# Pinning VectorE and TensorE to program order around the context's last rows, and starting the second matrix's GpSimd sums with the third feed pair

## The chip, the cores and the metric

The kernel runs on one core of one Trainium2 chip. The metric is the device time of one execution in microseconds (us). Before the change three runs gave 1945.74, 1946.46 and 1949.13 us; the median is 1946.46 us. One more execution was taken with the hardware profiler on.

The engines go by the profile's names: PE is the matrix engine (TensorE), PEld its weight loads, DVE is VectorE, ACT is ScalarE, POOL is GpSimd, SP is SyncE, which here only issues transfers. ACT and POOL issue transfers too.

## The reference

One layer of a diffusion backbone works on 1024 latent tokens and 256 context tokens, both 1024 channels wide. The change touches only the end of the first half and the feed-forward block:

```python
x = x + gt1 * (merged @ w_out)
u2 = rmsnorm(x, g_norm2) * (1 + sc2) + sh2
x = x + gt2 * (jnp.square(jax.nn.relu(u2 @ w_ff1)) @ w_ff2)
```

Here `w_out` is 1024 x 1024, `w_ff1` is 1024 x 4096 and `w_ff2` is 4096 x 1024, all in float32. The scales, shifts and gates (`sc2`, `sh2`, `gt1`, `gt2`) differ between context and latent tokens.

## The kernel before

**Numbers in two halves.** Every matrix operand is split into a rounded half `h` and a rest `l`. ACT casts the `h`; DVE subtracts to get the `l`. Each product is then three matmuls: `h·h`, `h·l`, `l·h`. A split of one 128 x 512 tile is thus one ACT cast and one DVE subtraction.

**Tokens.** The ten row tiles of 128 tokens form three groups: group 0 (tiles 0 to 3), group 1 (tiles 4 to 7), both latent, and group 2 (tiles 8 and 9), the context.

**Output projection.** `project_out` (L1158) forms, for one row tile and one range of columns, 24 matmuls into a PSUM bank `po`. DVE multiplies by the gate (L1171) and adds to the rows `z` (L1173); ACT squares the sum and leaves a row sum in `fsq` (L1174). For the context the columns come in four quarters `q` of 256. `context_out(q)` (L1178) first fetches and splits four weight tiles (`raw_wc`, `hi_wc`, `lo_wc`; L879 to L882), then calls `project_out` for tiles 8 and 9. The raw tiles have 4 buffers (`first4`), the `h` halves 6 (`six`) and the `l` halves 6 (`ring`).

**Normalised columns.** `modulate_ff(g)` (L1118) sums `fsq` (DVE, `fs`, L1122), makes the reciprocal root (`rs_f`: DVE L129, then POOL L130), scales the rows (`xn`: even tiles on ACT L1134, odd tiles on DVE L1136), transposes them on PE into PSUM (`pt`, L1142; five banks of the kind `sd`), and evicts. For groups 0 and 1 ACT evicts to `u2r` (L1151) and DVE splits some of them (`u2h`, `u2l`, L1154 and L1155). For the context ACT works inside PSUM (L1146), and DVE takes both halves from there (`u20c` to `u27c`: a cast at L1147 and a subtraction at L1148 for each of eight column blocks, two blocks to a quarter `qt`).

**Feed-forward, first matrix.** A `Pair` takes two of the 32 blocks of `w_ff1` and the latent tokens as a 2 x 2 block product with seven half-size products instead of eight. The right sides are four quarters of `u2`, `B11`, `B21`, `B12`, `B22`, and four sums of them, `T1` to `T4`. Each quarter has four tiles, `kk` = 0 to 3. `quarter_sums` (L780) overwrites the raw quarters by the sums, 4 DVE subtractions for each `kk`, and `split_sum` (L789, L790) splits them, 4 for each sum. A pair goes through `begin` (the products with `B11` and `B21`, `fB`), `contexts` (the context tokens, `fc`; it splits the quarters `a21` and `a22` of the weights), `rest` (DVE differences of weights at L947, splits `s_...` at L872 and L873, the products `fT` with `T4`, `T2`, `T3`, `T1` and one with `B22`) and `sums` (DVE L1227 to L1230, stores `scr_h`, `scr_c`, `scr_s`). In the profile `a_0l` is the `l` half of a weight quarter of pair 0, `s_0l` that of a difference. The raw weights of a pair lie in one of two places, so a pair's load (L905) waits for the last split of the pair two before it.

**Feed-forward, second matrix.** `second_sums(fp)` (L1235) makes the same kind of sums of `w_ff2`: two loads by SP into one place (`z` 16 to 19; L1239), four POOL subtractions (L1242), one store by POOL (`scr_t`, L1243). The next call's loads wait until that store has landed. The sums are read in the second half of the feed-forward block only.

**What sets the order.** The Tile framework puts the instructions of each engine in one fixed queue when the kernel is built. It takes them by readiness in a modelled run, and by program order among the ready. An engine's queue is then worked in that order, and an instruction that waits holds up all behind it. `Pinned(tc, engine)` (L33) is a wrapper that the kernel already uses in its first part: each instruction issued through it is put in the engine's queue behind the instruction that the program issued last on that engine, pinned or not. It orders the queue and adds no wait for that instruction's end. Instructions issued without the wrapper may still be placed anywhere between.

Around the change the program reads: `context_out(0)`, `context_out(1)`, `modulate_ff(1)`, `context_out(2)`, `context_out(3)`, then `begin` of pairs 0 and 1, `modulate_ff(2)`, all quarter sums, the splits in the order `T4`, `T3`, `T2`, `T1`, `contexts` of pairs 0 and 1, and then for each of 16 pairs `rest`, `sums` and `second_sums`, with no pinning.

Of the kernel before, what the change touches and what calls it, by code (L numbers as in the profile page):

```python
# [48 lines left out]
def hybrid_step(  # L49
# [1065 lines left out]

    fsq = cp.tile([P, NT, 4], F32, name="fsq")

    def modulate_ff(g):  # L1118
        t0, n = GROUPS[g]
        tiles = range(t0 // P, (t0 + n) // P)  # L1120
        fs = small([P, 4], f"fs{g}")[:, : len(tiles)]
        V.reduce_sum(fs, fsq[:, tiles[0] : tiles[-1] + 1, 0 : 4 if g == 2 else 2], axis=mybir.AxisListType.X)  # L1122
        r = rstd_of(fs, len(tiles), f"f{g}")

        j = 1 if g == 2 else 0
        for qt in range(4):
            xn = []
            for ii, i in enumerate(tiles):
                if ii % 2 == 0:
                    t = tmp2(f"xn{i}_{qt}")  # L1130
                v = t[:, (ii % 2) * 256 : (ii % 2) * 256 + 256]
                xv = xt[i][:, qt * 256 : (qt + 1) * 256]
                if ii % 2 == 0:
                    A.activation(v, xv, AF.Copy, scale=r[:, ii : ii + 1])  # L1134
                else:
                    V.tensor_scalar(v, xv, r[:, ii : ii + 1], None, ALU.mult)  # L1136
                xn.append(v)
            for kk in range(2):
                k = qt * 2 + kk
                ps = ps_sd(f"pt2{g}_{k}")  # L1140
                for ii in range(n // P):
                    PE.transpose(ps[:, ii * P : (ii + 1) * P], xn[ii][:, kk * P : (kk + 1) * P], ident)  # L1142
                if g == 2:
                    c = slot(f"u2{k}c")
                    u2c[k] = hi, lo = c[:, 0:256], c[:, 256:512]
                    A.activation(ps[:, :n], ps[:, :n], AF.Identity, bias=sh2[:, k, j : j + 1], scale=a2[:, k, j : j + 1])  # L1146
                    V.tensor_copy(hi, ps[:, :n])  # L1147
                    V.tensor_tensor(lo, ps[:, :n], hi.bitcast(F32), ALU.subtract)  # L1148
                    continue
                rf = raw2[g][k] = slot(f"u2r{k}_{g}", F32)  # L1150
                A.activation(rf, ps[:, :n], AF.Identity, bias=sh2[:, k, j : j + 1], scale=a2[:, k, j : j + 1])  # L1151
                if g == 0 or k >= 4:
                    hi, lo = slot(f"u2h{k}_{g}"), slot(f"u2l{k}_{g}")
                    V.tensor_copy(hi, rf)  # L1154
                    V.tensor_tensor(lo, rf, hi.bitcast(F32), ALU.subtract)  # L1155
                    u2s[f"B{1 + k // 4}{1 + g}", k % 4] = hi, lo

    def project_out(tiles, c0, n, weights):  # L1158

        for i in tiles:  # L1160
            g = min(i // 4, 2)
            o = i * P - GROUPS[g][0]
            full = ps_mm(f"po{c0}_{i}")
            ps = full[:, :n]
            for k in range(KT):
                whi, wlo = weights(k)
                mh, ml = mT[k][g]
                PE.matmul(ps, mh[:, o : o + P], whi, start=k == 0, stop=False)  # L1168
                PE.matmul(ps, ml[:, o : o + P], whi, start=False, stop=False)
                PE.matmul(ps, mh[:, o : o + P], wlo, start=False, stop=k == KT - 1)  # L1170
            V.tensor_tensor(ps, ps, gt1[(2 if g == 2 else 0) + c0 // 512][:, c0 % 512 : c0 % 512 + n], ALU.mult)  # L1171
            xc = xt[i][:, c0 : c0 + n]
            V.tensor_tensor(xc, xc, ps, ALU.add)  # L1173
            A.activation(ps, xc, AF.Square, accum_out=fsq[:, i, c0 // n : c0 // n + 1])  # L1174
            if c0 + n == D:
                SP.dma_start(scr_x[i], xt[i])

    def context_out(q):  # L1178
        ws = context_weights(q)
        project_out((8, 9), q * 256, 256, lambda k: tuple(w[:, k % 2 * 256 : k % 2 * 256 + 256] for w in ws[k // 2]))  # L1180

# [2 lines left out]
    project_out(range(5), 512, 512, lambda k: w_out1[k])  # L1186
    modulate_ff(0)
    project_out(range(5, 8), 512, 512, lambda k: w_out1[k])
    context_out(0)
    context_out(1)  # L1190
    modulate_ff(1)
    quarters = (("B11", 0, 0), ("B21", 0, 4), ("B12", 1, 0), ("B22", 1, 4))
    raw2q = {nm: raw2[g][o : o + 4] for nm, g, o in quarters}
    context_out(2)
    context_out(3)

# [43 lines left out]
            G.tensor_tensor(out, x, y, ALU.subtract)  # L1242
        G.dma_start(scr_t[fp], zs(16, 4).rearrange("p (q c) -> p q c", c=512))  # L1243


    pairs = {}

    def feed_pair(fp):
        odd = fp % 2
        pairs[fp] = FeedPair(  # L1250
            f"{fp}", fp, (w_ff1[2 * fp], w_ff1[2 * fp + 1]), 4 if odd else 0, range(8, 12) if odd else range(12, 16), u2s, u2c)

    for fp in (0, 1):
        feed_pair(fp)
        pairs[fp].begin()
    modulate_ff(2)
    quarter_sums(raw2q)
    for nm in ("T4", "T3", "T2", "T1"):
        split_sum(u2s, raw2q, nm)
    for fp in (0, 1):  # L1260
        pairs[fp].contexts()
    for fp in range(NFP):
        if fp not in pairs:
            feed_pair(fp)
            pairs[fp].begin()
            pairs[fp].contexts()
        pairs[fp].rest()
        pairs[fp].sums()
        del pairs[fp]
        second_sums(fp)  # L1270


    pa.close()
# [262 lines left out]
```

## Time and profile before

| | us |
|---|---|
| median of three runs | 1946.46 |
| the profiled execution's own time | 1947.31 |
| its span, first to last instruction | 1945.5 |
| PE busy in it | 1903.0 |
| DVE busy | 1294.0 |
| ACT busy | 861.7 |
| POOL busy | 378.2 |

The profiled execution's time exceeds its span by 1.8 us, and the median of the runs by 0.85 us. All times of instructions below count from the start of the span. The projection of the context's rows starts at 1118.5 us, the feed pairs begin at 1145.0 us, and the second matrix's products run from about 1556 us to the end.

### The profile page before, as it was taken

What the parts mean: (1) busy time and instruction counts of PE and PEld (TensorE: products, weight loads), DVE (VectorE), ACT (ScalarE), POOL (GpSimd) and SP (SyncE); (2) the same over time, 40 slices, a digit from 0 to 9 for tenths busy, and PEclk for the clock granted to TensorE, in tenths of its full rate; (3) what the DMA queues carried; (4) which work ended last, traced back from release to release, by engine and by line L of the source; (5) the groups of instructions that cost most, each with busy time, mean ns of one, the idle gap of its engine ahead of it and who ended that gap; (6) DMA issues with size and microseconds to landing.
All of it is one profiled execution on the core that took longest, in us unless ns stands there. A gap on an engine that the chain in (4) does not pass through costs nothing.

```text
span 1945.5 us, 28129 instructions
## 1 busy us (share of the span) xinstructions
PE 1903.0 (98%) x10136; PEld 1627.5 (84%) x10136; DVE 1294.0 (67%) x2207; ACT 861.7 (44%) x1768; POOL 378.2 (19%) x380
## 2 busy tenths in 40 slices
PE   6999999999999999999999999999999999999998
PEld 3778888998788888888888887888888888888886
DVE  6574443347759889875675599888776655744665
ACT  7444464653243333343123374555454545443443
POOL 1200001107302424220000015444431110000003
PEclk9999999999999999999999999999999999999999
DMA  9211111012635445469522435776773586654444
GB/s 361 85 59 33 43 39 40 27 56 70 203 119 165 149 158 164 153 211 321 163 97 98 152 120 212 253 264 246 259 269 136 193 333 203 210 170 151 165 133 159
DMA packets 149318, 313.32 MB, mean 161 GB/s; under 512 B 17550, under 2 KB 40818, under 8 KB 147130
## 3 DMA queue, kind: packets, MB, share of 16 engines
q1 hardware_dynamic: 107354, 220.73, 33.9%
q0 software_dynamic: 15520, 57.75, 7.8%
q10 hardware_dynamic: 26304, 33.04, 4.7%
q8 instruction: 79, 1.29, 0.3%
q14 instruction: 61, 0.50, 0.1%
HBM read 217.59 MB, written 93.36 MB: 160 GB/s over the span
## 4 chain that ended last, share of the span: by engine, by line
PE 87%; DVE 4%; DMA 3%; POOL 2%; ACT 1%; issue 1%; SPq 0%; POOLq 0%; ACTq 0%; DVEq 0%
PE w L1403 6%; PE w L1404 6%; PE w L1405 6%; PE pb L1050 3%; PE pb L1051 3%; PE pb L1052 3%; PE fT L892 3%; PE fT L890 3%; PE fT L891 3%; PE fB L891 2%; PE fB L890 2%; PE fB L892 2%; PE fT_g L892 2%; PE fT_g L890 2%; PE fT_g L891 2%; PE po L1168 2%
## 5 line engine op out<-in xcount | busy, mean ns | idle before, releaser
L1242 POOL TENSOR_TENSOR z<-z 128x512 f32<-128x512 f32 x64 | 100.1, 1564 | 123.3 <-DMA z<-in_w_ff 120.6
L947 DVE TENSOR_TENSOR z<-z 128x512 f32<-128x512 f32 x112 | 88.7, 792 | 2.5
L527 POOL PARTITION_ALL_REDUCE acc<-acc x16 | 54.6, 3446 | 184.0 <-DVE acc L521 113.6
L521 DVE SCALAR_TENSOR_TENSOR acc<-z,scond,acc 128x512 f32<-128x512 f32 x112 | 86.1, 816 | 0.0
L1357 POOL TENSOR_TENSOR rs_y<-rs_y,neghalf 128x1 f32<-128x1 f32 x10 | 9.6, 966 | 333.0 <-DVE rs_y L1356 333.0
L1208 ACT ACTIVATE z<-z 128x512 f32<-128x512 f32 x64 | 40.5, 632 | 69.8 <-DVE z L956 36.7
L972 ACT ACTIVATE z<-z 128x512 f32<-128x512 f32 x48 | 30.3, 632 | 59.1 <-DVE z L956 23.1
L130 POOL TENSOR_TENSOR rs_h<-rs_h,neghalf 128x4 f32<-128x4 f32 (+1 forms) x12 | 10.9, 910 | 200.5 <-DVE rs_h L129 200.3
L653 DVE SCALAR_TENSOR_TENSOR yc<-th,ccol,z 128x512 f32<-128x512 f32 (+1 forms) x12 | 7.9, 661 | 58.2 <-PE th L651 58.2
L1056 DVE TENSOR_TENSOR sg<-pb,sg 128x512 f32<-128x512 f32 (+1 forms) x48 | 28.7, 600 | 26.7 <-PE pb L1052 26.5
L881 ACT CAST hi_wb<-raw_wb 128x512 fp32r<-128x512 f32 x24 | 14.8, 620 | 64.4 <-PE pb L1051 37.6
L1209 ACT ACTIVATE z<-z 128x512 f32<-128x512 f32 x64 | 40.3, 629 | 1.1
L1171 DVE TENSOR_TENSOR po<-po,gt 128x512 f32<-128x512 f32 (+1 forms) x24 | 14.6, 607 | 35.1 <-PE po L1170 35.0
L1233 POOL DMA_DIRECT2D scr_s<-x x48 | 26.3, 549 | 53.1 <-DVE x L1227 47.6
L738 POOL TENSOR_TENSOR z<-z 128x1024 f32<-128x1024 f32 (+13 forms) x20 | 33.6, 1702 | 6.9 <-ACT z L722 4.6
L528 POOL TENSOR_TENSOR acc<-acc,bt 1x512 f32<-1x512 f32 x16 | 23.5, 1480 | 58.4 <-issue 58.4
L1174 ACT ACTIVATE po<-z 128x512 f32<-128x512 f32 (+1 forms) x24 | 12.7, 529 | 48.5 <-DVE z L1173 34.2
L587 DVE SCALAR_TENSOR_TENSOR z<-z,dmb,kv 128x129 f32<-128x129 f32 x56 | 16.6, 345 | 21.8 <-PE kv L576 21.3
L1057 DVE TENSOR_TENSOR z<-z,sg 128x512 f32<-128x512 f32 (+1 forms) x48 | 28.7, 601 | 1.2
L640 DVE TENSOR_TENSOR den<-den,gcol 128x2 f32<-128x2 f32 x40 | 6.2, 159 | 31.0 <-ACT den L639 29.9
L43 PE MATMUL pm<-wah,shl 128*4 128x512 f32 x32 | 13.8, 461 | 13.2 <-ACT wah L43 13.2
L130 POOL TENSOR_TENSOR rs_f<-rs_f,neghalf 128x4 f32<-128x4 f32 (+1 forms) x3 | 3.3, 1092 | 116.9 <-DVE rs_f L129 116.9
(5136 smaller groups left out, 7288.9 us busy)
## 6 DMA issues: line engine op xcount, KB each, us to landing
z<-in_w_ff SPq DMA_DIRECT2D x64, 512.0 KB, 5.5
z<-in_w_ada SPq DMA_DIRECT2D x64, 256.0 KB, 3.1
scr_t<-z POOLq DMA_DIRECT2D x16, 1024.0 KB, 4.9
z<-in_w_in SPq DMA_DIRECT2D x24, 512.0 KB, 4.3
scr_g<-z ACTq DMA_DIRECT2D x48, 256.0 KB, 2.0
sg<-scr_g SPq DMA_DIRECT2D x48, 256.0 KB, 4.5
scr_h<-z ACTq DMA_DIRECT2D x48, 256.0 KB, 3.6
scr_s<-x POOLq DMA_DIRECT2D x48, 256.0 KB, 4.3
```

The source lines that it names most:

```text
L521: V.scalar_tensor_tensor(acc[j], raw, scond[:, k, j : j + 1], acc[j], ALU.mult, ALU.add)
L890: PE.matmul(ps, whi[:, s], ahi, start=first and k == ks[0], stop=False)
L891: PE.matmul(ps, whi[:, s], alo, start=False, stop=False)
L892: PE.matmul(ps, wlo[:, s], ahi, start=False, stop=end and k == ks[-1])
L947: V.tensor_tensor(out, x, y, op)
L1050: PE.matmul(pb[:, :n], whi[:, s], yh, start=kc == 0, stop=False)
L1051: PE.matmul(pb[:, :n], whi[:, s], yl, start=False, stop=False)
L1052: PE.matmul(pb[:, :n], wlo[:, s], yh, start=False, stop=kc == 3)
L1242: G.tensor_tensor(out, x, y, ALU.subtract)
L1403: PE.matmul(banks[j], h_[:, s], rh, start=fp == 0, stop=False)
L1404: PE.matmul(banks[j], l_[:, s], rh, start=False, stop=False)
L1405: PE.matmul(banks[j], h_[:, s], rl, start=False, stop=fp == NFP - 1)
```

## The change

The calls after `modulate_ff(1)` are put in another order, and some are pinned:

1. The raw weights of pairs 0 and 1 and the context weights of quarters 2 and 3 are requested and split first, unpinned.
2. With DVE and PE pinned: the rows of `context_out(2)`, the quarter sums for `kk` = 0, the rows of tile 8 of `context_out(3)`, the sums for `kk` = 1, the rows of tile 9.
3. With PE alone pinned: `begin` of pairs 0 and 1.
4. With DVE alone pinned: `modulate_ff(2)`, in which the sums for `kk` = 2 stand between the reciprocal root and the scaling of the rows; then the sums for `kk` = 3; then the splits in the order `T4`, `T2`, `T3`, `T1`.
5. In the loop over pairs SP is pinned, and no `second_sums` is called for pairs 0 and 1; pairs 2 and 3 call it twice, later pairs once, so all 16 are made.

```diff
-    def modulate_ff(g):
+    def modulate_ff(g, between=None):
...
         r = rstd_of(fs, len(tiles), f"f{g}")
+        if between:
+            between()
...
-    def project_out(tiles, c0, n, weights):
+    def project_out(tiles, c0, n, weights, between=None):
         for i in tiles:
+            if between and i == tiles[-1]:
+                between()
...
-    context_out(0)
-    context_out(1)
+    for q in (0, 1):
+        context_out(q, context_weights(q))
     modulate_ff(1)
...
-    context_out(2)
-    context_out(3)
...
     for fp in (0, 1):
         feed_pair(fp)
+
+    def row_sums(kk):
+        b11, b21, b12, b22 = (raw2q[nm][kk] for nm in ("B11", "B21", "B12", "B22"))
+        for out, x, y in ((b11, b12, b11), (b12, b22, b12), (b22, b22, b11), (b21, b22, b21)):
+            V.tensor_tensor(out, x, y, ALU.subtract)
+
+    wcs = [context_weights(q) for q in (2, 3)]
+    V, PE = Pinned(tc, engines[0]), Pinned(tc, engines[3])
+    context_out(2, wcs[0])
+    row_sums(0)
+    context_out(3, wcs[1], lambda: row_sums(1))
+    V = engines[0]
+    for fp in (0, 1):
         pairs[fp].begin()
-    modulate_ff(2)
-    quarter_sums(raw2q)
-    for nm in ("T4", "T3", "T2", "T1"):
+    PE = engines[3]
+    V = Pinned(tc, engines[0])
+
+    modulate_ff(2, lambda: row_sums(2))
+    row_sums(3)
+    for nm in ("T4", "T2", "T3", "T1"):
         split_sum(u2s, raw2q, nm)
+    V = engines[0]
     for fp in (0, 1):
         pairs[fp].contexts()
+    SP = Pinned(tc, nc.sync)
+    summed = 0
     for fp in range(NFP):
...
-        second_sums(fp)
+        for _ in range(min(2, fp + 1 - summed) if fp > 1 else 0):
+            second_sums(summed)
+            summed += 1
+    SP = nc.sync
```

More of the change, by code (lines that the diff above doesn't have):

```diff
@@ L1176, in project_out, with context_out @@
                 SP.dma_start(scr_x[i], xt[i])
-    def context_out(q):
-        ws = context_weights(q)
-        project_out((8, 9), q * 256, 256, lambda k: tuple(w[:, k % 2 * 256 : k % 2 * 256 + 256] for w in ws[k // 2]))
+    def context_out(q, ws, between=None):
+        project_out((8, 9), q * 256, 256, lambda k: tuple(w[:, k % 2 * 256 : k % 2 * 256 + 256] for w in ws[k // 2]), between)
     project_out(range(8), 0, 512, lambda k: w_out0[k])
```

## The prediction

> **What bounds the kernel now.** I read the page's first section, then the busy times by stage, then PE's waits from the context's rows to the end, and last each engine's order around those waits.
>
> ```profile
> PE 1903.0 (98%) x10136; PEld 1627.5 (84%) x10136; DVE 1294.0 (67%) x2207; ACT 861.7 (44%) x1768; POOL 378.2 (19%) x380
> ```
>
> PE is busy for 98% of the span, and the change removes no matmul. It can only win back idle time of PE, or add some. The stages (span in us; busy us of PE, PEld, DVE, ACT, POOL; PE clock; DMA share; GB/s) show where that lies:
>
> ```profile
> 1118.00:1145.00 27.00, 27.00 (x228) 26.88 (x227) 24.96 (x54) 21.54 (x46) 1.52 (x1) 1.00 0.38 118
> 1145.00:1160.00 15.00, 11.97 (x54) 9.73 (x53) 13.24 (x28) 8.58 (x21) 0.70 (x1) 0.96 0.26 105
> 1160.00:1190.00 30.00, 27.91 (x165) 23.72 (x164) 29.26 (x51) 18.56 (x39) 17.73 (x8) 0.96 0.45 155
> 1190.00:1235.00 45.00, 42.65 (x210) 35.28 (x209) 39.93 (x55) 22.43 (x42) 21.66 (x24) 1.00 0.72 262
> 1235.00:1560.00 325.00, 325.00 (x1724) 281.16 (x1723) 242.08 (x357) 166.53 (x309) 118.11 (x134) 1.00 0.65 231
> ```
>
> PE has no idle time up to 1145, loses 3.03 us before 1160, 2.09 before 1190 and 2.35 before 1235, and none from there to 1560. All that can be won where the change acts is 7.5 us, and what the lowered clock costs (0.04 of 45 us, 1.8 us). From 1160 to 1190 DVE is busy for 29.26 of 30 us: there DVE sets the pace. PE's waits agree:
>
> ```profile
> PE pt L1142 <- ACT xn L1134: 3.0, 1, 3.0
> PE fT L890 <- ACT s_0h L872: 0.9, 3, 0.4
> PE fT L892 <- DVE s_2l L873: 0.9, 1, 0.9
> PE fT L892 <- DVE s_0l L873: 0.3, 1, 0.3
> ```
>
> The largest is the wait for the context's scaled rows; the rest are short waits for splits by ACT and DVE.
>
> **Part 1: PE behind the transposes of group 1.** The first pinned matmul, of `context_out(2)`, stands behind the last instruction issued on PE, the last transpose of `modulate_ff(1)`. Before, PE filled the gaps between those transposes with that quarter's matmuls:
>
> ```profile
> 1130.03 2.35 PE L1142 MATMUL pt<-cst,xn 128*128 128x128 f32 x20
> 1132.13 0.36 PE L1168 MATMUL po<-hi_wc,m0c 128*128 128x256 f32 x1
> 1137.03 0.60 PE L1142 MATMUL pt<-cst,xn 128*128 128x128 f32 x4
> ```
>
> ```profile
> 1133.89 0.60 ACT L872 CAST a_0h<-z 128x512 fp32r<-128x512 f32 x1
> 1134.40 0.78 ACT L1151 ACTIVATE u2r<-pt,sh,a 128x512 f32<-128x512 f32 x1
> ```
>
> Twenty transposes, five of eight blocks with a PSUM bank each, take 2.10 us to the next start, 0.42 a block. The other three wait for a bank, so for ACT. The eighth needs ACT's third eviction, the one at 1134.40, which ends near 1135.1; were ACT to leave out the cast at 1133.89 and one like it before, a step of 0.51 us each, 1134.1. The last block then ends at 1134.5 to 1135.5, against 1133.4 for a PE that never stops. I take the middle, **+1.6 us**. The bounds are 0 (ACT keeps up) and +4.1 (the last block stays at 1137.03: 4.90 us less two blocks). Behind it wait all matmuls of quarters 2 and 3 and both `begin`.
>
> Pinning DVE costs nothing at this place: its first row product stands behind quarter 3's last weight split, which waits for buffers until PE is in the second tile of quarter 2, but PE has three `po` banks and goes on. If that cover failed, PE would wait a row's two operations and a square, some 1.5 us, within part 1's bounds.
>
> **Part 2: the wait before the context's transposes.** The row sum `fs` is the first instruction pinned after `begin`, so it stands behind DVE's last one there, L927 of pair 1, which waits for PE's last `fB` matmul. Earlier rows are thus of no use to it.
>
> ```profile
> 1155.59 0.15 DVE L1122 TENSOR_REDUCE fs<-fsq 128x2 f32<-128x8 f32 x1
> 1156.12 0.69 DVE L927 TENSOR_TENSOR z<-z,fB 128x512 f32<-128x512 f32 x1 [0.38 <-PE fB L892]
> 1157.33 0.16 DVE L129 TENSOR_SCALAR rs_f<-fs 128x2 f32<-128x2 f32 x1
> 1158.30 1.14 DVE L1136 TENSOR_SCALAR xn<-z,rs_f 128x256 f32<-128x256 f32 x4 [0.81 <-POOL rs_f L130]
> 1160.71 0.42 DVE L1147 CAST u20c<-pt 128x256 fp32r<-128x256 f32 x1 [1.27 <-ACT pt L1146]
> ```
>
> ```profile
> 1157.57 0.70 POOL L130 TENSOR_TENSOR rs_f<-rs_f,neghalf 128x2 f32<-128x2 f32 x1 [33.16 <-DVE rs_f L129]
> ```
>
> ```profile
> 1159.12 1.11 PE L1142 MATMUL pt<-cst,xn 128*128 128x128 f32 x4 [3.03 <-ACT xn L1134]
> ```
>
> After: L927 at the same place, `fs` 0.6 us later at 1156.7, the root's two steps until about 1157.9. DVE meanwhile makes the sums for `kk` = 2:
>
> ```profile
> L780 DVE TENSOR_TENSOR u2r<-u2r,u2r 128x512 f32<-128x512 f32 x16 | 10.8, 681 | 0.0
> ```
>
> At DVE's usual step of 0.6 us (the start of `fs` behind L927 counts the same) four of them end at 1159.5. They stand ahead of DVE's first `xn`, which then lets the second tile's transpose start at 1159.9 and the first cast at about 1160.7, where it was. The wait stays, at **0** more or less; bounds -0.5 and +1.2 (four sums of which none is hidden, less the 1.27 that DVE sat idle there). All times of parts 2 and 3 lie later by part 1.
>
> **Part 3: the context's halves in written order.** Before, DVE scaled all four quarters at once (1158.30, x4) and then ran 16 casts and subtractions without a gap:
>
> ```profile
> 1165.81 0.41 DVE L1148 TENSOR_TENSOR u27c<-pt,u27c 128x256 fp32r<-128x256 f32 x1
> 1166.14 1.45 DVE L790 TENSOR_TENSOR T4l<-u2r,T4h 128x512 fp32r<-128x512 f32 x1
> 1167.52 1.77 DVE L873 TENSOR_TENSOR a_0l<-z,a_0h 128x512 fp32r<-128x512 f32 x1
> 1169.21 2.99 DVE L790 TENSOR_TENSOR T4l<-u2r,T4h 128x512 fp32r<-128x512 f32 x3
> 1172.12 0.68 DVE L873 TENSOR_TENSOR a_0l<-z,a_0h 128x512 fp32r<-128x512 f32 x1
> 1182.16 0.68 DVE L873 TENSOR_TENSOR s_0l<-z,s_0h 128x512 fp32r<-128x512 f32 x1
> ```
>
> ```profile
> 1160.17 2.93 ACT L1146 ACTIVATE pt<-pt,sh,a 128x256 f32<-128x256 f32 x6
> ```
>
> In the program the scaling of a quarter stands after the halves of the quarter before, and pinned it stays there. Each quarter now runs as a chain: scaling 0.3, two transposes 0.35, ACT 0.5, four DVE steps 1.6 (0.33 to 0.46 each), hand-offs 0.2: 3.0 us. The last subtraction ends at 1160.7 + 1.6 + 3 x 3.0 = 1171.3, not 1166.2: +5.1. PE's `fB` products show what it has to put there:
>
> ```profile
> 1145.01 0.40 PE L890 MATMUL fB<-u2h,a_0h 128*128 128x512 f32 x1
> 1155.69 0.39 PE L892 MATMUL fB<-u2h,a_1l 128*128 128x512 f32 x1
> ```
>
> These are the first and the last of 48, 0.227 us each. The 48 `fc` matmuls ready by then are half as wide, some 5.5 us, and `T4` waits: the pinned `kk` = 3 sums (4 x 0.6 = 2.4) and three `T2` splits that DVE had done before (1.8) now come first. Against this, DVE can put three splits of weights in the gaps (-1.8), and it no longer meets GpSimd:
>
> ```profile
> 1164.37 6.08 POOL L1242 TENSOR_TENSOR z<-z 128x512 f32<-128x512 f32 x4 [6.10 <-DMA z<-in_w_ff]
> 1178.57 13.34 POOL L1242 TENSOR_TENSOR z<-z 128x512 f32<-128x512 f32 x4 [7.20 <-DMA z<-in_w_ff]
> ```
>
> While the first four ran, DVE's splits took 1.45, 1.77 and 2.99 (three) instead of 0.68, 0.68 and 1.88: 3.0 us lost, now saved. The second four run until 1191.9, past PE's last wait of this stage, the one for `s_0l`; I count nothing. So `s_0l`, which PE waited for, comes 5.1 + 2.4 + 1.8 - 1.8 - 3.0 = 4.5 us later. PE can cover at most pair 1's `T4` product, 12 matmuls of 0.227, 2.7 us; its weights are late too, so half: **+3.1 us**. Bounds: -2.1 (the idle time of 1160 to 1190 goes) and +8.
>
> The Trainium skill, "SBUF — State Buffer", section "Who interferes with whom", says that a VectorE instruction with two SBUF inputs and a GpSimd one that reads SBUF exclude each other for a whole instruction. By that rule the first four would have cost DVE their full 6.1 us, the term would be 0.0 and the sum +0.4; the rows show half of it, and they decide.
>
> **Part 4: GpSimd and SP later.** GpSimd's sums 0 and 1 move from 1164 and 1178 to after pair 2's load. Each pinned SP load of `w_ff2` stands ahead of the next pair's:
>
> ```profile
> 1184.27 3.44 SPq L905 DMA_DIRECT2D z<-in_w_ff  x2
> 1199.13 1.50 SPq L905 DMA_DIRECT2D z<-in_w_ff  x2
> 1227.78 0.93 SPq L905 DMA_DIRECT2D z<-in_w_ff  x2
> z<-in_w_ff SPq DMA_DIRECT2D x64, 512.0 KB, 5.5
> scr_t<-z POOLq DMA_DIRECT2D x16, 1024.0 KB, 4.9
> ```
>
> A round of load (5.5), sums (6.1) and store (4.9) lasts about 17 us, so two rounds between pairs 3 and 4 put pair 4's load at 1184 + 3 x 17 = 1235 instead of 1228. Its first use is later:
>
> ```profile
> 1249.91 0.28 PE L890 MATMUL fc<-u20c,a_4h 128*128 128x256 f32 x1
> ```
>
> With 5.5 us to land and two splits that leaves 8 us of cover; uncovered it would cost 7. The other loads keep their times, since one round fits in a pair's 25 us (325 us hold 13 pairs). DVE meets the moved sums from 1190 on, where PE still lost 2.35. With less traffic from the third round on I take back half, **-1.2 us**; bounds -2.35 and +3. In the steady part PE has no idle time to win.
>
> **The sum.** +1.6 + 0 + 3.1 - 1.2 = +3.5 us. On the profiled execution's 1947.31 that is 1950.8; the runs' median lies 0.85 lower, so I predict **1950.0**.
>
> **Rivals.** (B) *The last weight quarter's split is queued behind the pinned sum splits.* Before, it came after the four of `T4` (`a_0l` at 1172.12). Unpinned and later in the program, it can come after `T2` and `T3` too: eight splits of 0.6, 4.8 us more before PE's `T4` product. 1946.46 + 3.5 + 4.8 = 1954.8. For it: the sums are ready early. Against: ACT's casts of the sums need buffers and left DVE gaps before. Chance 0.22.
>
> (C) *Faster: DVE's freed time feeds PE.* Without GpSimd's eight instructions, and with `T2` ahead of `T3` as the products need them, both remaining idle stretches go: -2.09 - 2.35 = -4.4, 1942.0. It decides if `s_0l` is there when PE has run out, and part 1 is 0. For it: DVE lost 3.0 us in the first four alone. Against: parts 2 and 3, which only add. Chance 0.18.
>
> (D) *The change moves work but no wait:* parts 1 and 3 are both covered; 1946.5, within 1. For it: DVE has 6.6 us less to do before `begin` ends. Chance 0.10.
>
> **Chances and range.** My forecast (A, 0.50) has its own range from +0.5 to +6.5, 1947 to 1953. A difference under 0.2%, 3.9 us, can't be told from none here. A gives 0.29 to no change and 0.21 to slower, B 0.22 to slower, C 0.17 to faster and 0.01 to no change, D 0.10 to no change: faster 0.17, same 0.40, slower 0.43. The range takes in C and B with part 1's upper bound half used: 1941.5 to 1956.5.
>
> **What would show it.** Part 1: idle time of PE at `pt` near 1132 to 1135, none before. Part 2: `fs` right behind L927 of pair 1, and PE's wait for `xn` again about 3 us. Part 3: `xn` on DVE in four separate instructions with the halves between, the last near 1173, and DVE operations without the 1.77. Part 4: pair 4's load near 1235 or later. I am wrong if the transposes wait for nothing, if DVE's halves run on without gaps, or if PE waits over 2 us after 1235.

## The result, and the profile after

Five runs of the changed kernel gave a median of 1964.15 us (1962.42 to 1966.54), five of the kernel before 1949.13 us. The ratio is 1.0079, with a 95% interval of 1.0065 to 1.0093: the change costs 15.0 us. The prediction was 1950.0 us, 3.5 us above the median of 1946.46 that it started from, with a range that ended at 1956.5.

The busy times of the whole span (1962.4 us), from the first section of the page of the changed kernel:

```profile
PE 1910.5 (97%) x10136; PEld 1630.9 (83%) x10136; DVE 1309.0 (67%) x2207; ACT 861.3 (44%) x1768; POOL 378.1 (19%) x380
```

PE has the same 10136 matmuls. Its busy time grew by 7.5 us, mostly since some of them ran at a lowered clock, and its idle time by 9.4 us (52 instead of 42.5). The stages of the changed kernel, with the columns of the prediction's table:

```profile
1118.00:1145.00 27.00, 25.71 (x205) 24.65 (x204) 21.64 (x47) 20.99 (x43) 1.52 (x1) 1.00 0.39 132
1145.00:1160.00 15.00, 14.69 (x80) 12.44 (x78) 10.11 (x20) 6.99 (x17) 0.00 (x0) 1.00 0.22 89
1160.00:1190.00 30.00, 21.69 (x126) 17.84 (x126) 23.54 (x50) 18.51 (x40) 1.07 (x1) 0.89 0.06 21
1190.00:1235.00 45.00, 43.91 (x208) 36.62 (x209) 42.39 (x61) 22.21 (x41) 19.08 (x20) 0.96 0.61 225
1235.00:1300.00 65.00, 60.51 (x307) 51.76 (x306) 47.48 (x63) 26.40 (x52) 31.63 (x31) 0.95 0.70 250
1300.00:1560.00 260.00, 260.00 (x1379) 224.88 (x1378) 208.74 (x287) 133.15 (x248) 97.77 (x105) 1.00 0.63 231
```

Two stages lose time. From 1160 to 1190 PE is idle for 8.3 us at a mean clock of 0.89, and DVE, which was busy for 29.26 of these 30 us before, for only 23.54. From 1235 to 1300, where PE had no idle time before, it is idle for 4.5 us at a mean clock of 0.95.

To compare kernels I use one figure, the **lost time**: in windows of 5 us from 1115 to 1320, PE's idle time plus the missing share of the clock times 5 us, added up. Before, it is 7.5 + 1.7 = 9.2 us; after, 15.5 + 8.5 = 24.0 us. The difference of 14.8 us is close to the 15.0 us between the medians, and it lies in these places: 1115 to 1145 +1.3, 1145 to 1190 +5.2, 1190 to 1235 +0.4, 1235 to 1320 +7.9.

The figure is good to about 2 us. Where PE is idle while its clock is lowered, it counts the same time twice: 1.9 us after and 0.2 us before, 1.3 of the 1.9 behind 1235. And it stands for one execution of each kernel. The spans of the two lie 16.9 us apart, and 1.7 of that was there when the projection of the context's rows began (1120.2 instead of 1118.5), ahead of all that the change touches. Start times from two kernels differ by that much before anything else.

PE's waits from 1118 to 1330 of the changed kernel name them (us in total, times, longest):

```profile
PE fc L890 <- ACT a_4h L872: 4.3, 1, 4.3
PE pt L1144 <- ACT xn L1136: 2.8, 1, 2.8
PE fT L890 <- ACT s_0h L872: 1.7, 3, 1.1
PE pt L1144 <- ACT u2r L1153: 1.3, 2, 0.7
PE fc L890 <- DVE u24c L43: 1.2, 1, 1.2
PE fc L890 <- DVE u26c L43: 1.0, 1, 1.0
PE fc L890 <- DVE u22c L43: 0.9, 1, 0.9
PE fc L890 <- DVE u20c L43: 0.9, 1, 0.9
```

The wait for `xn` was there before. New are the four waits for the context's halves, one for each quarter, the wait for `u2r` of group 1, and the largest, for the weights of pair 4. DVE's queue after the change (start, duration, instruction; in brackets the idle time before it and what ended it; pinned instructions carry the wrapper's line, L43):

```profile
1159.79 0.69 DVE L927 TENSOR_TENSOR z<-z,fB 128x512 f32<-128x512 f32 x1 [4.42 <-PE fB L43]
1160.40 0.15 DVE L43 TENSOR_REDUCE fs<-fsq 128x2 f32<-128x8 f32 x1
1160.67 2.86 DVE L43 TENSOR_TENSOR u2r<-u2r,u2r 128x512 f32<-128x512 f32 x4
1163.44 0.35 DVE L43 TENSOR_SCALAR xn<-z,rs_f 128x256 f32<-128x256 f32 x1
1164.93 0.42 DVE L43 CAST u20c<-pt 128x256 fp32r<-128x256 f32 x1 [1.14 <-ACT pt L1148]
...
1166.52 0.34 DVE L43 TENSOR_SCALAR xn<-z,rs_f 128x256 f32<-128x256 f32 x1
1169.59 0.43 DVE L43 CAST u22c<-pt 128x256 fp32r<-128x256 f32 x1 [2.73 <-ACT pt L1148]
...
1171.18 0.35 DVE L43 TENSOR_SCALAR xn<-z,rs_f 128x256 f32<-128x256 f32 x1
...
1174.63 0.35 DVE L43 TENSOR_SCALAR xn<-z,rs_f 128x256 f32<-128x256 f32 x1
...
1177.47 0.42 DVE L43 TENSOR_TENSOR u27c<-pt,u27c 128x256 fp32r<-128x256 f32 x1
...
1198.61 0.69 DVE L873 TENSOR_TENSOR s_0l<-z,s_0h 128x512 fp32r<-128x512 f32 x1
```

`fs` stands right behind L927, and the four scalings stand apart, each behind the halves of the quarter before. DVE stands idle between them. From 1145 to 1190 it is idle for 11.4 us (15.00 - 10.11 + 30.00 - 23.54), 2.5 before. Of this, 4.4 us lie ahead of L927 of pair 1, for which everything pinned behind it waits, and 6.0 us in four waits between the quarters (1.14, 2.73, 0.91 and 1.24). This work is still to be done, so the last `s_0l` of pair 0 moved from 1186.17 to 1198.61. The line before:

```profile
1186.17 1.19 DVE L873 TENSOR_TENSOR s_0l<-z,s_0h 128x512 fp32r<-128x512 f32 x1
```

Behind it waits SP's first pinned load, for 43.5 us; two lines from other engines show the end of that row:

```profile
1199.32 55.15 SPq L43 DMA_DIRECT2D z<-in_w_ff  x14
```

```profile
1262.75 1.14 ACT L872 CAST a_4h<-z 128x512 fp32r<-128x512 f32 x2 [7.26 <-DMA z<-in_w_ff]
```

The load for pair 2 starts 0.7 us behind that split, at 1199.32 instead of 1184.27. It is two transfers, one for each half of the weights. Before, the planner put first the half that needs only an earlier split, so its start at 1184.27 lay 1.9 us ahead of the last split. In written order the half that waits for the last split comes first. Pair 4's weights, behind it and behind two rounds of the second matrix, are cast at 1262.75; before, the first cast of them came here:

```profile
1240.21 0.62 ACT L872 CAST a_4h<-z 128x512 fp32r<-128x512 f32 x1 [2.24 <-PE fc L891]
```

### The profile page after: what moved, and what is told of

The parts are those of the page before. It is cut to its first block, busy times and chain, and to the rows that moved or that the text cites. A ratio compares the mean times of both kernels' runs of the same rounds, so it can differ in the third digit from the quotient of the medians.

```text
span 1962.4 us, 28119 instructions
## 1 busy us (share of the span) xinstructions
PE 1910.5 (97%) x10136; PEld 1630.9 (83%) x10136; DVE 1309.0 (67%) x2207; ACT 861.3 (44%) x1768; POOL 378.1 (19%) x380
## 4 chain that ended last, share of the span: by engine, by line
PE 81%; DVE 7%; issue 4%; DMA 4%; ACT 2%; POOL 1%; SPq 0%; POOLq 0%; DVEq 0%; ACTq 0%
PE w L1428 6%; PE w L1429 6%; PE w L1430 6%; PE pb L1050 3%; PE pb L1051 3%; PE pb L1052 3%; PE fT L892 3%; PE fT L890 3%; PE fT L891 3%; PE fB L891 2%; PE fB L890 2%; PE fB L892 2%; PE fT_g L892 2%; PE fT_g L890 2%; PE fT_g L891 2%
## 5 line engine op out<-in xcount | busy, mean ns | idle before, releaser
L1243 POOL TENSOR_TENSOR z<-z 128x512 f32<-128x512 f32 x64 | 95.6, 1493 | 86.8 <-DMA z<-in_w_ff 83.8
L947 DVE TENSOR_TENSOR z<-z 128x512 f32<-128x512 f32 x112 | 109.4, 976 | 2.5
L1232 POOL DMA_DIRECT2D scr_c<-xc x16 | 11.6, 724 | 122.5 <-DVE xc L1231 112.2
L43 PE MATMUL pm<-wah,shl 128*4 128x512 f32 x32 | 13.8, 460 | 13.8 <-DVE s_x L43 12.5
```

What stands on the lines that cost most here:

```text
L947: V.tensor_tensor(out, x, y, op)
```

## The experiments

Each diff is against the changed kernel, but for the first. The table sums up all runs: median, ratio to the kernel before with its 95% interval; then from the one profiled execution of each kernel: start of the context's projection and the time from there to the end of the span, start of the last `s_0l` on DVE, PE's first matmul on `a_4`, PE's wait for `a_4h`, and the lost time as idle time + clock. Each ratio is to runs of the kernel before taken beside that run (medians 1949.0 to 1949.6). The start of the context's projection lies ahead of every edit, and it still varies by 4.4 us between executions (1115.8 to 1120.2). So times of two kernels are compared below with the difference of their starts beside them.

| run | median, us | ratio | start + rest | `s_0l` | `a_4` | wait | lost, us |
|---|---|---|---|---|---|---|---|
| before | 1949.1 | | 1118.5 + 827.0 | 1186.2 | 1249.9 | 0 | 7.5 + 1.7 |
| after | 1964.2 | 1.0079 [1.0065, 1.0093] | 1120.2 + 842.2 | 1198.6 | 1263.4 | 4.3 | 15.5 + 8.5 |
| tail_only | 1946.3 | 0.9987 [0.9978, 0.9996] | 1119.9 + 827.0 | 1186.9 | 1252.5 | 1.8 | 7.0 + 3.4 |
| sp_free | 1962.6 | 1.0071 [1.0052, 1.0089] | 1119.9 + 840.4 | 1201.5 | 1263.4 | 0 | 12.5 + 8.6 |
| ctx_dve_free | 1947.0 | 0.9988 [0.9978, 0.9998] | 1118.4 + 824.1 | 1184.1 | 1247.9 | 0 | 5.9 + 0 |
| pe_free | 1963.2 | 1.0077 [1.0057, 1.0097] | 1115.8 + 842.1 | 1192.2 | 1258.3 | 5.6 | 16.0 + 10.2 |
| halves_last | 1958.0 | 1.0038 [1.0025, 1.0051] | 1119.4 + 834.0 | 1192.0 | 1257.0 | 2.5 | 10.4 + 5.2 |
| sums_free | 1957.6 | 1.0035 [1.0021, 1.0049] | 1117.9 + 837.9 | 1192.6 | 1259.2 | 3.0 | 12.6 + 6.9 |
| both | 1953.1 | 1.0019 [1.0009, 1.0029] | 1118.1 + 834.1 | 1188.5 | 1255.2 | 3.1 | 9.8 + 6.9 |
| load_first | 1955.5 | 1.0028 [1.0017, 1.0039] | 1118.8 + 833.0 | 1197.0 | 1256.2 | 0 | 10.8 + 3.5 |
| ctx_free | 1944.6 | 0.9973 [0.9961, 0.9984] | 1118.1 + 823.7 | 1182.7 | 1247.8 | 1.5 | 6.1 + 1.7 |
| ctx_free_load | 1946.0 | 0.9985 [0.9976, 0.9993] | 1118.1 + 826.5 | 1182.8 | 1243.0 | 0 | 3.5 + 1.7 |
| ctx_free_no_tail | 1949.8 | 1.0007 [0.9998, 1.0017] | 1119.6 + 828.7 | 1188.1 | 1251.9 | 0 | 7.4 + 3.4 |
| scaled_ahead | 1943.3 | 0.9969 [0.9958, 0.9981] | 1118.7 + 821.8 | 1182.0 | 1242.5 | 0 | 3.1 + 0 |

### Which pin costs

**tail_only**: the kernel before, with the part of the change in the pair loop alone.

```diff
+    SP = Pinned(tc, nc.sync)
+    summed = 0
     for fp in range(NFP):
...
-        second_sums(fp)
+        for _ in range(min(2, fp + 1 - summed) if fp > 1 else 0):
+            second_sums(summed)
+            summed += 1
+    SP = nc.sync
```

> The kernel before with the last part of the change alone: SP in written order from the feed-forward loop on, and the second matrix's sums from the third pair on, two rounds in each of the first rounds. Theory (two separate causes; here the second, pair 4's weights queued behind two rounds of the second matrix's load, sums and store): PE waits about 4 us for a_4h, runs at a granted clock near 0.66 behind it, and the time rises by 4 to 7 us, to 1953-1956 beside a kernel before of 1949. Rival (the tail only hurts because the context's rows left DVE late, so that every load came 15 us late): no wait for a_4h over 1 us, and the time stays within 2 us of 1949.

Measured: not slower but 0.13% faster than before. There is a wait for `a_4h`, of 1.8 us and without a drop of the clock, and PE lost nothing from 1190 to 1235 (2.35 before). My theory of two separate causes fell: the tail alone costs nothing. The rival was nearer, though the time is lower than it had and the wait longer. The gain shows in the medians only: from its start the profiled execution takes as long as that of the kernel before (827.0 us).

**sp_free**: SP is left to the planned order.

```diff
-    SP = Pinned(tc, nc.sync)
     summed = 0
```

> The changed kernel with SP left to the planned order; the sums are still written from the third pair on. Theory: the second matrix's loads are planned early again, pair 4's weights are not behind two rounds, PE's wait of 4.3 us for a_4h is gone with the clock's dip behind it, and the time falls by 5 to 7 us from 1964 to 1957-1959. Rival (the wait for a_4h only swallows lateness that DVE's part brought, and the loss turns up elsewhere): 1962-1964, with waits of the same sum at other places in 1180 to 1300.

Measured: the rival's result. The wait for `a_4h` is gone, but the time is within the uncertainty of the changed kernel's. The planner puts the second matrix's first sums early again, and now they meet DVE's late work. DVE's queue there, instructions that took over 0.9 us each, and GpSimd at that time:

```profile
1179.95 1.78 DVE L873 TENSOR_TENSOR a_0l<-z,a_0h 128x512 fp32r<-128x512 f32 x1
1181.66 1.79 DVE L43 TENSOR_TENSOR u2r<-u2r,u2r 128x512 f32<-128x512 f32 x1
1183.37 1.38 DVE L1230 TENSOR_TENSOR xc<-hc 128x128 f32<-128x128 f32 x1
```

```profile
1179.46 5.13 POOL L1243 TENSOR_TENSOR z<-z 128x512 f32<-128x512 f32 x3 [10.93 <-DVE u2r L43]
```

Of DVE's instructions the first two take 0.68 us each elsewhere, the third 0.28. PE waits 1.6 us for `T4l`, and the lost time from 1165 to 1235 is 15.3 us instead of 10.1. One loss was exchanged for another.

**ctx_dve_free**: DVE is pinned around the output projection only, and free from the context's `fs` on; PE and SP stay pinned.

```diff
     PE = engines[3]
-    V = Pinned(tc, engines[0])
     modulate_ff(2, lambda: row_sums(2))
```

> The changed kernel with VectorE left to the planned order from the context's scaling on (fs, the four xn, the halves, the last row sums and the sum splits); around the output projection of the context's rows it stays pinned, and so do the matrix engine and SP. Theory: the four scalings stand together again ahead of the halves, T4's first product on a_0 starts 5 to 7 us earlier than in the changed kernel (1179.0), and the time falls by 5 to 9 us to 1955-1959. Rival (written order on the matrix engine is what delays the context): T4's first product stays within 2 us of 1179 and the time within 2 us of 1964.

Measured: one line takes back all of the loss, more than the theory had. DVE's queue:

```profile
1158.23 0.16 DVE L1122 TENSOR_REDUCE fs<-fsq 128x2 f32<-128x8 f32 x1 [0.19 <-ACT po L1178]
1159.41 1.14 DVE L1138 TENSOR_SCALAR xn<-z,rs_f 128x256 f32<-128x256 f32 x4 [0.81 <-POOL rs_f L130]
1160.47 0.68 DVE L927 TENSOR_TENSOR z<-z,fB 128x512 f32<-128x512 f32 x1
...
1167.33 0.42 DVE L1150 TENSOR_TENSOR u27c<-pt,u27c 128x256 fp32r<-128x256 f32 x1
```

`fs` and the four scalings stand ahead of L927 of pair 1, and the last half starts at 1167.33 instead of 1177.47 (1.8 us of that lie ahead of the start). The eight late row sums were made between 1134 and 1150, before the projection was done. PE's longest wait from 1118 to 1330 is 1.4 us, and its clock never drops. SP is pinned with the same rounds, and no wait for `a_4h` is left. So the 7.9 us lost behind 1235 in the changed kernel need the pinned SP **and** DVE's lateness; with the pinned SP alone, in tail_only, 2.8 us are lost there.

**pe_free**: PE is left to the planned order.

```diff
-    V, PE = Pinned(tc, engines[0]), Pinned(tc, engines[3])
+    V = Pinned(tc, engines[0])
...
-    PE = engines[3]
```

> The changed kernel with the matrix engine left to the planned order; VectorE and SP stay pinned. Theory: the matrix engine's pin costs only what the transposes of group 1 make it wait ahead of the context's last product (3.6 us of later fB, of which 1.7 was there before the change's place): the time falls by 1 to 3 us to 1961-1963. Rival (the matrix engine's written order is the main cause, through the product of pair 1 on B21 standing ahead of the transposes): T4 starts 5 us earlier or more and the time falls to 1955-1958.

Measured: no difference from the changed kernel. `T4`'s first product comes 6.4 us earlier, but 4.4 of that lie ahead of the start, so only 2.0 are the edit's, and the rival fell by its own measure, too. Nothing is won: against the changed kernel PE loses 1.3 us less up to 1145, 3.4 more from there to 1165, 3.4 less to 1235 and 3.5 more behind that, where the wait for `a_4h` grows to 5.6 us, with 5.1 us lost to the clock.

### What in DVE's written order costs

**halves_last**: DVE stays pinned, but the context's four scalings are written ahead of the halves.

```diff
+        if g == 2:
+            for qt in range(4):
+                scaled(qt)
         for qt in range(4):
-            xn = []
-            for ii, i in enumerate(tiles):
...
+            if g != 2:
+                scaled(qt)
+            xn = xns[qt]
```

> The changed kernel, VectorE still pinned, but written in another order: the context's four scalings first, then the halves quarter by quarter; the row sums and sum splits keep their written places. Theory (the chain by quarters is the cost: scaling of a quarter behind the halves of the one before, 3 us each): the four xn stand together near 1163.5 to 1164.6, the last half is done near 1171 instead of 1177.9, T4's first product on a_0 comes 4 to 7 us earlier than 1179.0, the clock's dips of 1160 to 1170 shrink, and the time is 1951-1955. Rival (the eight sums pinned ahead of and behind the scaling, 2.86 and 2.4 us, are the cost): T4's first product comes less than 3 us earlier and the time stays at 1959-1963.

Measured: 6.1 us faster than the changed kernel, between the two theories' times. The four scalings stand together at 1162.40, the last half starts at 1169.92, and `T4`'s first product comes 5.3 us earlier (1173.76), 0.8 of it ahead of the start. So the chain by quarters is a cause, but not the whole.

**sums_free**: the row sums of `kk` = 2 and 3 and the sum splits are unpinned; `fs`, scaling and halves stay pinned quarter by quarter.

```diff
-    modulate_ff(2, lambda: row_sums(2))
+    modulate_ff(2)
+    V = engines[0]
+    row_sums(2)
     row_sums(3)
     for nm in ("T4", "T2", "T3", "T1"):
         split_sum(u2s, raw2q, nm)
-    V = engines[0]
```

> The changed kernel with the last two rows' sums (eight subtractions) and the sum splits left to the planned order, and the context's fs, scaling and halves still pinned quarter by quarter. Theory (chain by quarters): the sums go earlier into gaps, which takes about 2 us from the first xn and 2.4 us from the splits, and the chain of four quarters stays with a last half 11 to 14 us behind the first xn: T4's first product 3 to 5 us earlier, time 1957-1960. Rival (the pinned sums are the cost): T4's first product at 1170-1173 and the time 1950-1954.

Measured: the theory's time, 6.6 us below the changed kernel, but not by its way: `T4`'s first product comes only 0.3 us earlier (1178.70), and since the start lay 2.3 us earlier, it comes 2.0 later from there. What moved is DVE's backlog behind it: the last `s_0l` is 6.0 us earlier, 3.7 from the start.

**load_first**: each pair's weights are loaded ahead of the rounds of the second matrix that are written behind the pair before.

```diff
         if fp not in pairs:
             feed_pair(fp)
+        if fp > 1:
             pairs[fp].begin()
...
+        if 1 < fp < NFP - 1:
+            feed_pair(fp + 1)
         for _ in range(min(2, fp + 1 - summed) if fp > 1 else 0):
```

> The changed kernel with the next pair's weights loaded (and only loaded) ahead of the rounds of the second matrix that are written behind the pair; SP stays pinned. Theory (pair 4's weights behind two rounds are a cost of their own, once everything is late): the wait of 4.3 us for a_4h and the dip of 3.4 us behind it are gone, and the time falls by 5 to 8 us to 1956-1959. Rival (as with SP left free, where that wait went and 1.5 us were won: the lateness turns up as another wait): 1961-1964, with a lost time (idle and dip) in 1115 to 1320 still over 21 us.

Measured: 8.6 us faster than the changed kernel. The stage from 1235 to 1300 loses nothing: the first two casts of `a_4h` are done by 1250, PE comes at 1256.2 and waits for nothing. The rival fell. Together with ctx_dve_free this shows the last 7.9 us to be one thing, weights queued behind two rounds that had started late.

**both**: the edits of halves_last and sums_free at once.

> The changed kernel with both edits at once: the context's four scalings written ahead of the halves, and the last two rows' sums and the sum splits in planned order; fs, scaling and halves stay pinned behind L927 of pair 1, the matrix engine and SP stay pinned. Each edit alone won 6 to 6.5 us of the loss of 15 (medians 1964.2 to 1949). Theory (the written order costs by how late the last s_0l is on VectorE: the rounds on SP start 0.7 us behind it and bring pair 4's weights to a first use 64 to 66 us behind it, whatever the matrix engine does): the last s_0l is at 1185-1188, a_4's first use at 1250-1253, a wait for a_4h under 2 us without a dip, and with the wait of 2.8 us for xn still there the time is 1949-1952. Rival (the two edits win the same microseconds): s_0l at 1191 or later, 1955-1958.

Measured: 1953.1 us, one microsecond above the theory's range. By the medians the two edits nearly add up (6.1 + 6.6 against 11.0 us), and the rival fell; but `a_4h` is still waited for, 3.1 us, with 3.4 us of clock. The profiled execution, the slowest of ten, doesn't show the adding up: from its start it takes as long as that of halves_last (834 us). In all runs with SP pinned and the rounds ahead of the load, `a_4` is first used 64 to 67 us behind the last `s_0l` (the table's columns). With the load ahead it is 59 to 61 us, and nothing is waited for. I read the first figure as what the queue on SP takes, two rounds and the load, and the second as what PE needs; this is a reading and not shown, since in ctx_dve_free PE comes 63.8 us behind and waits for nothing. How much of the 5 us is a wait depends on what other products the planned order gives PE meanwhile, and `s_0l` alone doesn't tell it. In this run a split that isn't pinned stands among the pinned halves and waits for ACT, holding DVE's queue:

```profile
1167.10 0.41 DVE L43 CAST u25c<-pt 128x256 fp32r<-128x256 f32 x1
1170.33 0.69 DVE L873 TENSOR_TENSOR a_0l<-z,a_0h 128x512 fp32r<-128x512 f32 x1 [2.81 <-ACT a_0h L872]
1170.94 0.42 DVE L43 TENSOR_TENSOR u25c<-pt,u25c 128x256 fp32r<-128x256 f32 x1
```

The 6 us between this run and ctx_dve_free go with the pin of `fs` behind L927, this stall and the wait for `a_4h`; I didn't take them apart.

### What is left of the change when nothing is pinned but SP

**ctx_free**: neither DVE nor PE is pinned anywhere; the written order of the calls, the order of the splits and the loop with SP pinned stay. (The expectation has DVE pinned around the output projection. In the kernel that ran it isn't.)

```diff
-    V, PE = Pinned(tc, engines[0]), Pinned(tc, engines[3])
...
-    PE = engines[3]
-    V = Pinned(tc, engines[0])
```

> The changed kernel with VectorE pinned only around the output projection of the context's rows and the first two rows' sums, the matrix engine free everywhere, SP pinned. Theory: with the context's scaling free there is no loss to win back but the 1.4 us that the pinned matrix engine waited for group 1's u2r; the four xn stand together; time 1944-1947, at or below the kernel before (1949). Rival (the planned order of the matrix engine puts pair 1's product on B21 ahead of the transposes, and fs comes later than with the pinned engine): a wait of 3 us at pt for xn and a dip behind it, as before the change: 1948-1951.

Measured: 0.27% faster than the kernel before, within the theory's range. The wait at `pt` is 3.0 us again, as the rival had it, and 1.7 us of clock go with it; the gain comes from behind it, where PE loses 0.35 us from 1165 to 1235 instead of 4.3.

**ctx_free_no_tail**: ctx_free with SP in planned order and `second_sums(fp)` in each pair, as before the change.

> As ctx_free, with SP in planned order and the second matrix's sums in each pair, as in the kernel before: of the change only the written place of the row sums and the order T4, T2, T3, T1 are left. Theory (the first GpSimd subtractions of the second matrix lengthen VectorE's halves and splits in 1178 to 1192, and the deferral saves this): 2 to 4 us slower than ctx_free, 1946-1949, with VectorE instructions of 1.77 us again. Rival (that contention is hidden by the matrix engine): within 1 us of ctx_free.

Measured: the kernel before's time. The gain is thus that of the deferral with SP pinned, and it is larger than the theory had it: 5.2 us by the medians, 5.0 from the start in the profiled executions. DVE and GpSimd in this run:

```profile
1169.41 1.79 DVE L873 TENSOR_TENSOR a_0l<-z,a_0h 128x512 fp32r<-128x512 f32 x1
1171.12 2.97 DVE L790 TENSOR_TENSOR T4l<-u2r,T4h 128x512 fp32r<-128x512 f32 x3
```

```profile
1166.20 6.15 POOL L1243 TENSOR_TENSOR z<-z 128x512 f32<-128x512 f32 x4 [6.88 <-ACT pt L1148]
```

Without them, in ctx_free, the three splits of `T4` took 1.88 us, and the last `s_0l` came 5.3 us earlier, 1.5 of it ahead of the start.

**ctx_free_load**: ctx_free with the edit of load_first.

> As ctx_free (VectorE and the matrix engine in planned order, SP pinned, the second matrix's sums from the third pair on), and the next pair's weights loaded ahead of the rounds of the second matrix. Theory: the wait of 1.5 us for a_4h is gone, time 1942.5-1944 beside ctx_free's 1944.6. Rival: the wait for hc (1.2 us) grows by as much: the same time within 0.5 us.

Measured: neither. The wait for `a_4h` is gone, but the last pair now waits 2.0 us for `s_15h` near 1540, with 1.7 us of clock, and a product of the second matrix 1.3 us for `accU`. The time is 1.4 us above ctx_free's, and the intervals overlap.

**scaled_ahead**: ctx_free_load, and on DVE `fs`, the root and the four scalings are pinned ahead of L927 of pairs 0 and 1. `begin(False)` leaves out L927, which is now `add()`; `modulate_ff` calls `adds` between the scaling and the transposes.

```diff
     for fp in (0, 1):
-        pairs[fp].begin()
+        pairs[fp].begin(False)
+    def adds():
+        nonlocal V
+        for fp in (0, 1):
+            pairs[fp].add()
+        V = engines[0]
+        row_sums(2)
+    V = Pinned(tc, engines[0])
+    modulate_ff(2, adds)
```

> The changed kernel with VectorE and the matrix engine in planned order again, the next pair's weights loaded ahead of the rounds, and the context's fs, rstd and four scalings pinned ahead of L927 of pairs 0 and 1 on VectorE. (The run ctx_free, like this one, left VectorE free around the output projection too, not only behind it as its text on record has it.) Theory: the wait of 3.0 us at pt for xn came from fs's product with D standing behind L927 of pair 1; with the scaling ahead of it the wait and the dip of 1.7 us behind it go, and the wait of 1.5 us for a_4h with them: 6 us below ctx_free, 1938-1941. Rival (fs is late by the context's own chain of the projection's last rows, not by L927): the wait stays at 2-3 us, time 1943-1946.

Measured: the wait at `pt` fell to 1.4 us and the clock stayed up, the smallest lost time of all. The time, 1943.3 us, is the lowest of all runs, 0.31% below the kernel before. It isn't the 1938 to 1941 expected, and can't be told from ctx_free's. Against ctx_free_load, run beside it and without this edit, it is 2.8 us lower. This version beats both kernels.

## Why the prediction was wrong

**Bound.** That PE bounds the kernel, and that the stage from 1160 to 1190 is DVE's, was right: what DVE lost there became PE's loss.

**Part 1** held. PE waits 1.3 us for `u2r` of group 1, and the first `fB` product comes 3.6 us later, of which 1.7 was there before the change's place and 1.95 is this part's, against +1.6. PE's wait for the evictions of ACT is what the part had named. Undone in pe_free it brought nothing: PE waited as long further on. The cover that the part saw for the pinned DVE held in the changed kernel. Where the late row sums are unpinned it failed: in ctx_dve_free, sums_free and both PE waits 1.4 us for a `po` bank until ACT has squared a row, near the 1.5 us that the part had named for that case.

**Part 2** held as far as it went: `fs` stands right behind L927 of pair 1, and the wait for `xn` is 2.8 us, as before. scaled_ahead showed what I hadn't asked: that place costs 1.6 us of wait and 1.7 us of clock in the kernel before, too.

**Part 3** had the right mechanism and was too small. The chain by quarters is there, with casts at 1164.93, 1169.59, 1173.05 and 1176.22: 4.7, 3.5 and 3.2 us apart, not 3.0. The first step is the long one; the clock is at 0.61 from 1165 to 1170, and PE's `fc` products of the first quarter, 0.22 us apart there instead of 0.12, stand ahead of the second quarter's last transposes (1168.57). The chain of the part had no product between a scaling and its transposes. I had the halves 5.1 us later and `s_0l` 4.5; measured against the lateness of 3.6 us that came in with `fB`, the last half is 8.1 us later and the last `s_0l` 8.8.

PE lost 5.2 us more from 1145 to 1190, against +3.1, and inside the bound of +8. Of the 5.2 us, 3.5 are idle time, near the +3.1, and 1.7 are clock. Two terms were missing. The wait for `xn`, as long as before, cost 3.4 us of clock and not 1.7. And the three weight splits with which I filled DVE's gaps didn't come there (one `a_0l` did): DVE was idle for 11.4 us instead of 2.5, 4.4 of them ahead of L927, where before it had made sums and `T2` splits. PE lost less than the 8.8 us by which `s_0l` was late, but the loads that wait for it were late in full.

The 6.1 us that the part names for a full exclusion of DVE and GpSimd are too many: up to 1166.14 DVE's instructions took an operand from PSUM and kept their 0.41 us, and the subtractions of two SBUF tiles that ran beside GpSimd after that took 0.8, 1.1 and (three together) 1.1 us longer. The rows don't contradict an exclusion for whole instructions.

**Part 4** is the step that failed. It put pair 4's load at 1184 + 3 x 17 = 1235, with 8 us of cover, and let "the other loads keep their times". But 1184 is when a split of pair 0 lets pair 2's load go, and part 3 had just made such splits 4.5 us late. The last split was 12.4 us late, and in written order the first transfer waits for that one and not for the one before it; the load started at 1199.3, 15 us late. The three rounds took 53.3 us, near the 51 of the part (their loads start at 1199.3, 1216.6 and 1238.1, the next one at 1252.6). So pair 4's load left at 1253.5 and not at 1235, and ACT had it 9.2 us later instead of 5.5. PE came for it 9.2 us later than before and still waited 4.3.

The 8 us of cover weren't there without the lateness either: in tail_only, with the last `s_0l` where it was within 0.7 us, PE waits 1.8 us for `a_4h`. Lateness came on top of a cover that was already used up. The price for that case was in the text, 7 us uncovered, and the stage lost 7.9; that the two are close is luck, since the wait itself was 4.3 us and the rest is clock, 1.3 us of it counted twice. Its bounds, -2.35 and +3, left that out.

The other half of this part was right, and its gain was estimated too low: alone the deferral won 2.8 us by the medians (tail_only), and with the calls in the new order 5.2 us (ctx_free against ctx_free_no_tail). The rows that go with it are DVE's subtractions beside GpSimd, up to 1.1 us longer each. The second four of GpSimd, for which the part counted nothing, lengthen them too: before, a subtraction at 1187.28 (L947) took 1.77 us.

**The rivals.** B's mechanism didn't come: the last weight quarter's split (`a_0l`, 1179.14) stands ahead of all four splits of `T4` (from 1181.75). What stands among the pinned sum splits are the splits of the differences, `s_0l`, and sums_free brought these forward. C, DVE's freed time feeding PE, was to give 1942.0; it is what ctx_free does, 1944.6, in which DVE isn't pinned, and scaled_ahead, 1943.3, in which it is pinned only from `fs` to L927. D, no wait moved, fell.

**The sum.** By the same places: part 1 +1.3 to 1.95 (+1.6 predicted), parts 2 and 3 +5.2 (+3.1), part 4 with the loads +0.4 + 7.9 (-1.2). The terms were treated as independent; the last one hung on the third, and its cover was taken too large.

## What to carry to other kernels

When a change makes one engine late and at the same time fixes the order of a queue that waits for that engine, the costs depend on one another: work out each wait behind the fixed queue again with the lateness of the part before, and check whether the cover that is left is still positive. Written order on an engine that sets the pace turns its waits into idle time, unless the program text already has the order that the data allow; here four scalings written ahead of the halves, and work without a deadline left unpinned, were worth 11 of 15 us. A deferral of work that can wait was a gain. A load that is needed next, put ahead of it, won 8.6 us where the queue had started late, and nothing where it hadn't (ctx_free_load).

## What the hardware showed that I had not expected

**The clock's second price.** A wait of PE near 3 us was followed by a stretch at a lowered clock. Two places in the changed kernel, in windows of 5 us:

```profile
1160.00:1165.00 5.00, 2.01 (x7) 1.07 (x7) 3.73 (x9) 3.60 (x8) 1.07 (x1) 0.71 0.14 52
1165.00:1170.00 5.00, 3.71 (x16) 3.37 (x16) 2.21 (x6) 1.33 (x3) 0.00 (x0) 0.61 0.00 0
...
1260.00:1265.00 5.00, 1.39 (x5) 1.10 (x5) 1.60 (x2) 2.25 (x5) 3.64 (x3) 0.61 0.49 197
1265.00:1270.00 5.00, 5.00 (x22) 4.46 (x22) 4.23 (x8) 1.03 (x3) 1.45 (x3) 0.71 0.63 247
```

Both times the two windows add up to (0.29 + 0.39) x 5 = 3.4 us of lost clock, at waits of 2.8 and 4.3 us. In windows of half a microsecond the clock is at 0.50 for about 6.8 us each time, the second time from 1261.2 on, 2.2 us before the wait ends. At the waits for `a_4h` of 1.5, 1.8 and 2.5 us nothing was lost, at 3.0 us 1.7, at 3.1 and 4.3 us 3.4 each, at 5.6 us 5.1. The wait for `xn`, 2.6 to 3.0 us long in twelve of the kernels, cost 1.7 us in three of them, 3.4 in seven and 5.1 in two (sp_free and sums_free). In ctx_dve_free and scaled_ahead, where no wait up to 1320 was over 1.4 us, the clock never dropped there. But one long wait isn't needed. In the changed kernel the clock dropped here, too:

```profile
1185.00:1190.00 5.00, 3.61 (x20) 2.53 (x18) 5.00 (x10) 4.16 (x10) 0.00 (x0) 1.00 0.23 70
1190.00:1195.00 5.00, 3.91 (x10) 2.61 (x11) 5.00 (x10) 2.17 (x4) 0.00 (x0) 0.78 0.12 34
```

PE was idle for 2.5 us of the 5 us from 1187.5 to 1192.5, in waits of at most 1.1 us, and the clock was at 0.50 from 1193 to 1196. So a wait of 3 us cost between 1.7 and 5.1 us more, as far as PE had work in that time.

The Trainium skill, "TensorE: Matmul & The Clock Gate", section "What's actually happening", has the clock at half rate behind an idle window of about 3.4 us, with a window that runs freely. The losses of 1.7, 3.4 and 5.1 us agree with one, two and three such windows at half rate. That they begin at waits of 2.6 to 3.0 us, and at several short waits in a row, differs from an idle window of that length, and here the rows decide; how much idle time within such a window is enough, no run here takes apart.

**DVE beside GpSimd.** In sp_free a DVE subtraction of 128 x 128 took 1.38 us instead of 0.28, and one of 128 x 512 took 1.78 instead of 0.68: 1.1 us more each, at both sizes.
